# Contrast adjustment on one core: rows of 32 KB in six buffers, stores on ScalarE's queue, clip in four pieces in a written-out order

## The chip, the cores and the metric

One core of a Trainium2 chip. The metric is the device time of the program in microseconds (us); lower is better. A profile's span is a little shorter than the measured time (238.6 us against 240.2 for the kernel before).

## The reference

48 images (16 x 3) of 512 x 512 fp32 pixels, 50.33 MB in and 50.33 MB out:

```python
def reference(x, factor):            # factor = 1.5
    mean = np.mean(x, axis=(2, 3), keepdims=True)
    return np.clip(mean + factor * (x - mean), 0, 1).astype(np.float32)
```

The mean of a whole image is needed before its first pixel can be written. So a tile is read once into on-chip memory, reduced, and changed in place.

## The kernel before

A tile holds 4 images as 128 partitions x 8192 columns (4 MB); eleven such tiles, then two tiles of 2 images (2 MB). VectorE sums each row, a matmul with a block matrix gives the bias `(1 - factor) * mean` on every partition of an image, ScalarE computes `relu(factor * x + bias)`, VectorE takes the minimum with 1.

```python
TILE_IMGS = [4] * 11 + [2, 2]
X_BUFS = 5
STORE_ENGINE = "gpsimd"
# ... pools, block matrices ...
for i, N in enumerate(TILE_IMGS):
    # ... xt, src, dst ...
    nc.sync.dma_start(out=xt, in_=src)
    rsum = rpool.tile([P, 1], f32)
    nc.vector.tensor_reduce(out=rsum, in_=xt, axis=mybir.AxisListType.X, op=mybir.AluOpType.add)
    pbias = psum.tile([P, 1], f32)
    nc.tensor.matmul(pbias, blockw[N], rsum, start=True, stop=True)
    bias = bpool.tile([P, 1], f32)
    nc.scalar.copy(out=bias, in_=pbias)
    nc.scalar.activation(out=xt, in_=xt, func=mybir.ActivationFunctionType.Relu, bias=bias, scale=factor)
    nc.vector.tensor_scalar(out=xt, in0=xt, scalar1=1.0, scalar2=None, op0=mybir.AluOpType.min)
    store_eng.dma_start(out=dst, in_=xt)
```

The order on each engine is not the order of this text: the scheduler of the language chooses it.

## Time and profile before

| kernel before | |
|---|---|
| measured time | 240.24 us median of three runs (240.1 to 240.93) |
| span of the profile | 238.6 us |
| bytes moved, mean rate | 100.66 MB, 422 GB/s |
| VectorE, ScalarE busy | 66%, 37% |

From the page of the kernel before: the span cut in 40 slices (a digit is the busy share in tenths, 9 is 90% or more; GB/s is what the DMA engines moved), then the three costliest groups (line, engine, operation, output<-input, count; busy us, mean ns of one; idle time of the engine just before, and what ended it). TENSOR_REDUCE is the row sum, called reduce below; ACTIVATE is the relu; TENSOR_SCALAR is the minimum with 1, called clip; L77 is line 77 of the kernel.

```profile
DVE  0088999999599079459629909917945979742300
...
DMA  7999999999999999999999999999999999999995
GB/s 269 434 439 439 439 439 352 439 434 439 439 439 439 439 434 434 423 428 412 423 439 439 434 439 439 439 439 439 434 428 426 426 404 428 431 434 439 428 434 214
...
L77 DVE TENSOR_REDUCE rsum<-xt 128x1 f32<-128x8192 f32 (+1 forms) x13 | 104.4, 8029 | 61.7 <-DMA xt<-in_x_dram 61.7
L90 ACT ACTIVATE xt<-xt,bias 128x8192 f32<-128x8192 f32 (+1 forms) x13 | 85.8, 6598 | 0.4
L97 DVE TENSOR_SCALAR xt<-xt 128x8192 f32<-128x8192 f32 (+1 forms) x13 | 53.2, 4091 | 5.0 <-ACT xt L90 5.0
```

The DMA row is the one that is full. At 439 GB/s, the commonest value of the slices (18 of 40), 100.66 MB take 229 us, so nearly all of the 238.6 us is transfer. VectorE waits 61.7 us for loads; beyond the 13 us of the first load this costs nothing, since the DMA engines are busy meanwhile.

Why VectorE and ScalarE stay hidden can be read from the timeline of the kernel before (start us, duration us, engine, line, operation):

```profile
13.03 8.69 DVE L77 TENSOR_REDUCE rsum<-xt 128x1 f32<-128x8192 f32 x1 [13.03 <-DMA xt<-in_x_dram]
...
22.64 7.12 ACT L90 ACTIVATE xt<-xt,bias 128x8192 f32<-128x8192 f32 x1
22.73 8.69 DVE L77 TENSOR_REDUCE rsum<-xt 128x1 f32<-128x8192 f32 x1 [1.02 <-DMA xt<-in_x_dram]
31.33 4.42 DVE L97 TENSOR_SCALAR xt<-xt 128x8192 f32<-128x8192 f32 x1
...
35.66 8.68 DVE L77 TENSOR_REDUCE rsum<-xt 128x1 f32<-128x8192 f32 x1
36.06 0.67 POOL L104 DMA_DIRECT2D out_dram<-xt  x1 [34.02 <-DVE xt L97]
```

ScalarE's 7.12 us ACTIVATE of tile 0 starts at 22.64. VectorE does not wait for it: at 22.73 it reduces tile 1, and only at 31.33 clips tile 0, by which time the ACTIVATE is over. The scheduler has put reduce(t+1) ahead of clip(t). So VectorE needs 8.69 + 4.42 = 13.1 us a tile, while the 8.4 MB that a tile moves (in and out) take 19.1 us at 439 GB/s.

The end of the timeline of the kernel before:

```profile
205.31 2.46 POOL L104 DMA_DIRECT2D out_dram<-xt  x1 [9.72 <-DVE xt L97]
205.36 2.29 DVE L97 TENSOR_SCALAR xt<-xt 128x4096 f32<-128x4096 f32 x1 [0.34 <-ACT xt L90]
207.95 0.53 POOL L104 DMA_DIRECT2D out_dram<-xt  x1 [0.18 <-issue]
...
223.49 0.53 POOL L104 DMA_DIRECT2D out_dram<-xt  x1 [15.00 <-DVE xt L97]
```

The last store, of 2 MB, is issued at 223.49, when older stores are still being moved. The DMA engines never run dry. (The store's issue on GpSimd that starts at 205.31 takes 2.46 us, the others 0.53 (the first of all 0.67); a 2.29 us clip on VectorE starts just after it.)

### The profile page before, as it was taken

The page shows a single profiled execution, that of the slowest core. Times are in us where ns is not written, and L with a number is a line of the kernel's source. Part 1 is how long each engine was busy: PE and PEld are TensorE (multiplying, and loading weights), DVE is VectorE, ACT ScalarE, POOL GpSimd, SP SyncE. Part 2 cuts the span into 40 slices and gives each one's busy share as a digit, 9 for nine tenths or more (in the row PEclk, how much of TensorE's full clock was granted, in tenths as well). Part 3 has the DMA queues.
Part 4 walks back from the last instruction along what each step waited for, and adds up shares of the span by engine and source line. Part 5 has one row for each costly group of instructions (what it writes and reads, how often), then busy time and mean ns, then how long its engine had stood idle before and what let it go on. Part 6 is the DMA issues. An engine that isn't in the chain of part 4 may idle for free.

```text
span 238.6 us, 238 instructions
## 1 busy us (share of the span) xinstructions
PE 7.4 (3%) x26; PEld 6.5 (3%) x26; DVE 156.5 (66%) x26; ACT 89.1 (37%) x27; POOL 10.3 (4%) x25
## 2 busy tenths in 40 slices
PE   0000000000000000000000000000000000000000
PEld 0000000000000000000000000000000000000000
DVE  0088999999599079459629909917945979742300
ACT  2002966472906601900920650470190095406000
POOL 2000001000000000000000000000000000500000
DMA  7999999999999999999999999999999999999995
GB/s 269 434 439 439 439 439 352 439 434 439 439 439 439 439 434 434 423 428 412 423 439 439 434 439 439 439 439 439 434 428 426 426 404 428 431 434 439 428 434 214
DMA packets 3744, 100.66 MB, mean 422 GB/s; under 512 B 416, under 2 KB 416, under 8 KB 416
## 3 DMA queue, kind: packets, MB, share of 16 engines
q1 hardware_dynamic: 1872, 50.33, 49.4%
q0 software_dynamic: 1872, 50.33, 49.0%
HBM read 50.33 MB, written 50.33 MB: 422 GB/s over the span
## 4 chain that ended last, share of the span: by engine, by line
issue 38%; DMA 35%; DVE 18%; POOL 2%; POOLq 0%; SPq 0%
DMA xt<-in_x_dram 19%; DMA out_dram<-xt 16%; DVE rsum L77 11%; DVE xt L97 7%; POOL out_dram L104 2%; POOLq L137 0%; SPq L74 0%; POOLq L104 0%
## 5 line engine op out<-in xcount | busy, mean ns | idle before, releaser
L77 DVE TENSOR_REDUCE rsum<-xt 128x1 f32<-128x8192 f32 (+1 forms) x13 | 104.4, 8029 | 61.7 <-DMA xt<-in_x_dram 61.7
L90 ACT ACTIVATE xt<-xt,bias 128x8192 f32<-128x8192 f32 (+1 forms) x13 | 85.8, 6598 | 0.4
L97 DVE TENSOR_SCALAR xt<-xt 128x8192 f32<-128x8192 f32 (+1 forms) x13 | 53.2, 4091 | 5.0 <-ACT xt L90 5.0
L88 ACT COPY bias<-pbias 128x1 f32<-128x1 f32 x13 | 2.1, 160 | 130.6 <-PE pbias L85 130.6
L104 POOL DMA_DIRECT2D out_dram<-xt x13 | 9.0, 692 | 213.0 <-DVE xt L97 212.8
L85 PE MATMUL pbias<-rsum,blockw 128*128 128x1 f32 x26 | 7.4, 355 | 209.5 <-DVE rsum L77 209.5
L85 PEld LDWEIGHTS pbias<-rsum,blockw 128*128 128x128 f32 x26 | 6.5, 311 | 210.3 <-DVE rsum L77 107.1
L88 ACT ACT_TABLE_LOAD x1 | 1.3, 1283 | 0.8 <-PEq L123 0.8
L51 POOL MEMSET blockw<- 32x32 f32 (+1 forms) x6 | 0.8, 128 | 0.2
L49 POOL MEMSET blockw<- 128x128 f32 x2 | 0.3, 205 | 0.3 <-POOLq L123 0.3
L123 POOL MEMSET const-float32-0.0<- 128x1 f32 x1 | 0.1, 104 | 0.2 <-issue 0.2
L123 POOL MEMSET const-bfloat16-1.0<- 128x1 bf16 x1 | 0.1, 113 | 0.0
L123 POOL MEMSET const-uint8-127<- 128x1 uint8 x1 | 0.1, 113 | 0.0
L123 POOL MEMSET const-float32-1.0<- 128x1 f32 x1 | 0.1, 110 | 0.0
## 6 DMA issues: line engine op xcount, KB each, us to landing
xt<-in_x_dram SPq DMA_DIRECT2D x11, 4096.0 KB, 24.6
out_dram<-xt POOLq DMA_DIRECT2D x11, 4096.0 KB, 36.0
xt<-in_x_dram SPq DMA_DIRECT2D x2, 2048.0 KB, 19.5
out_dram<-xt POOLq DMA_DIRECT2D x2, 2048.0 KB, 19.1
```

The source lines that it names most:

```text
L49: nc.gpsimd.memset(wt, 0.0)
L51: nc.gpsimd.memset(wt[b * PPI : (b + 1) * PPI, b * PPI : (b + 1) * PPI], wconst)
L77: nc.vector.tensor_reduce(out=rsum, in_=xt, axis=mybir.AxisListType.X, op=mybir.AluOpType.add,)
L85: nc.tensor.matmul(pbias, blockw[N], rsum, start=True, stop=True)
L88: nc.scalar.copy(out=bias, in_=pbias)
L90: nc.scalar.activation(out=xt, in_=xt, func=mybir.ActivationFunctionType.Relu, bias=bias, scale=factor,)
L97: nc.vector.tensor_scalar(out=xt, in0=xt, scalar1=1.0, scalar2=None, op0=mybir.AluOpType.min,)
L104: store_eng.dma_start(out=dst, in_=xt)
L123: nc = _bacc.Bacc("TRN2", target_bir_lowering=False, num_devices=1)
```

## The change

The intent as far as the code shows it: one more buffer, stores issued by a second hardware queue, and a clip in pieces so that VectorE clips a piece while ScalarE is at the next. The order is written out by hand, and each engine is held to it. The core of the diff:

```diff
-TILE_IMGS = [4] * 11 + [2, 2]
-X_BUFS = 5
-STORE_ENGINE = "gpsimd"
+P = 128
+ROW = 8192
+BUFS = 6
+CHUNK = 2048
 ... (pools and block matrix cut)
+    def load(t):
+        xt = xpool.tile([P, ROW], f32, name="xt")
+        nc.sync.dma_start(out=xt, in_=dram(x_f, t))
+        tiles[t] = xt
+    def compute(t):
+        xt = tiles[t]
+        ... (rsum, matmul, bias as before)
+        for c in range(0, ROW, CHUNK):
+            part = xt[:, c : c + CHUNK]
+            nc.scalar.activation(out=part, in_=part, func=Act.Relu, bias=bias, scale=factor)
+            nc.vector.tensor_scalar(out=part, in0=part, scalar1=1.0, scalar2=None, op0=Alu.min)
+    def store(t):
+        nc.scalar.dma_start(out=dram(out_f, t), in_=tiles.pop(t))
+    with tc.manual_schedule():
+        for t in range(min(BUFS, n_tiles)):
+            load(t)
+        for t in range(n_tiles):
+            compute(t)
+            store(t)
+            if t + BUFS < n_tiles:
+                load(t + BUFS)
```

There are now 12 tiles of 4 MB, so the last store is 4 MB. In the part cut here, the pools for sum, bias and matmul result also shrink (from 12, 12 and 8 buffers to 2 each).

More of the change, by code (lines that the diff above doesn't have):

```diff
@@ L5 @@
 import concourse.tile as tile
-from concourse import bass_utils, mybir
+from concourse import mybir
 from concourse._compat import with_exitstack
-TILE_IMGS = [4] * 11 + [2, 2]
-X_BUFS = 5
-STORE_ENGINE = "gpsimd"
+P = 128
+ROW = 8192
+BUFS = 6
+CHUNK = 2048
 @with_exitstack
@@ L23 @@
     nc = tc.nc
-    P = 128
+    f32 = mybir.dt.float32
+    Alu = mybir.AluOpType
+    Act = mybir.ActivationFunctionType
     B, C, H, W = x.shape
-    n_img = B * C
-    n_pix = H * W
+    n_img, n_pix = B * C, H * W
+    ppi = n_pix // ROW
+    per_tile = P // ppi
+    n_tiles = n_img // per_tile
+    assert ppi * ROW == n_pix and per_tile * n_tiles == n_img
     factor = float(factor)
-    f32 = mybir.dt.float32
-    assert sum(TILE_IMGS) == n_img
-    NMAX = max(TILE_IMGS)
+    wconst = (1.0 - factor) / float(n_pix)
@@ L36, with dram @@
     x_f = x.rearrange("b c h w -> (b c h w)")
     out_f = out.rearrange("b c h w -> (b c h w)")
-    wconst = (1.0 - factor) / float(n_pix)
+    def dram(ap, t):
+        return bass.AP(tensor=ap.tensor, offset=t * P * ROW, ap=[[ROW, P], [1, ROW]])
     consts = ctx.enter_context(tc.tile_pool(name="consts", bufs=1))
-    blockw = {}
-    for N in sorted(set(TILE_IMGS)):
-        wt = consts.tile([P, P], f32, name=f"blockw{N}")
-        PPI = P // N
-        if N == 1:
-            nc.gpsimd.memset(wt, wconst)
-        else:
-            nc.gpsimd.memset(wt, 0.0)
-            for b in range(N):
-                nc.gpsimd.memset(wt[b * PPI : (b + 1) * PPI, b * PPI : (b + 1) * PPI], wconst)
-        blockw[N] = wt
@@ L54 @@
-    xpool = ctx.enter_context(tc.tile_pool(name="xpool", bufs=X_BUFS))
-    rpool = ctx.enter_context(tc.tile_pool(name="rpool", bufs=12))
-    bpool = ctx.enter_context(tc.tile_pool(name="bpool", bufs=12))
-    psum = ctx.enter_context(tc.tile_pool(name="psum", bufs=8, space=bass.MemoryType.PSUM))
-    if STORE_ENGINE == "sync":
-        store_eng = nc.sync
-    elif STORE_ENGINE == "act":
-        store_eng = nc.scalar
-    else:
-        store_eng = nc.gpsimd
-    pix_off = 0
-    for i, N in enumerate(TILE_IMGS):
-        FREE = n_pix * N // P
-        npix_tile = n_pix * N
-        xt = xpool.tile([P, NMAX * n_pix // P], f32, name="xt")[:, :FREE]
-        src = bass.AP(tensor=x_f.tensor, offset=pix_off, ap=[[FREE, P], [1, FREE]])
-        dst = bass.AP(tensor=out_f.tensor, offset=pix_off, ap=[[FREE, P], [1, FREE]])
-        nc.sync.dma_start(out=xt, in_=src)
-        rsum = rpool.tile([P, 1], f32)
-        nc.vector.tensor_reduce(
-            out=rsum,
-            in_=xt,
-            axis=mybir.AxisListType.X,
-            op=mybir.AluOpType.add,
-        )
-        pbias = psum.tile([P, 1], f32)
-        nc.tensor.matmul(pbias, blockw[N], rsum, start=True, stop=True)
-        bias = bpool.tile([P, 1], f32)
-        nc.scalar.copy(out=bias, in_=pbias)
-        nc.scalar.activation(
-            out=xt,
-            in_=xt,
-            func=mybir.ActivationFunctionType.Relu,
-            bias=bias,
-            scale=factor,
-        )
-        nc.vector.tensor_scalar(
-            out=xt,
-            in0=xt,
-            scalar1=1.0,
-            scalar2=None,
-            op0=mybir.AluOpType.min,
-        )
-        store_eng.dma_start(out=dst, in_=xt)
-        pix_off += npix_tile
@@ new lines @@
+    xpool = ctx.enter_context(tc.tile_pool(name="xpool", bufs=BUFS))
+    rpool = ctx.enter_context(tc.tile_pool(name="rpool", bufs=2))
+    bpool = ctx.enter_context(tc.tile_pool(name="bpool", bufs=2))
+    psum = ctx.enter_context(tc.tile_pool(name="psum", bufs=2, space=bass.MemoryType.PSUM))
+    blockw = consts.tile([P, P], f32, name="blockw")
+    nc.gpsimd.memset(blockw, 0.0)
+    for a in range(0, P, ppi):
+        nc.gpsimd.memset(blockw[a : a + ppi, a : a + ppi], wconst)
+    tiles = {}
@@ new lines, in load @@
+    def load(t):
[4 more added lines that the diff above has]
+        xt = tiles[t]
+        rsum = rpool.tile([P, 1], f32, name="rsum")
+        nc.vector.tensor_reduce(out=rsum, in_=xt, axis=mybir.AxisListType.X, op=Alu.add)
+        pbias = psum.tile([P, 1], f32, name="pbias")
+        nc.tensor.matmul(pbias, blockw, rsum, start=True, stop=True)
+        bias = bpool.tile([P, 1], f32, name="bias")
+        nc.scalar.copy(out=bias, in_=pbias)
+        for c in range(0, ROW, CHUNK):
+            part = xt[:, c : c + CHUNK]
+            nc.scalar.activation(out=part, in_=part, func=Act.Relu, bias=bias, scale=factor)
+            nc.vector.tensor_scalar(out=part, in0=part, scalar1=1.0, scalar2=None, op0=Alu.min)
```

## The prediction

> **What bounds the kernel now.** The DMA engines: the page's slice rows show DMA at 9 tenths in 38 of 40 slices and mostly 439 GB/s; 100.66 MB at 439 GB/s is 229 us of the 238.6 us span. The rest is start and tail: the last store (2 MB) is issued at 223.5, the span ends 15 us later. VectorE (66% busy) and ScalarE (37%) are hidden: the scheduler puts reduce(t+1) before clip(t); in the timeline the reduce at 22.73 runs beside ScalarE's 7.12 us ACTIVATE of the tile before, and the clip follows at 31.33. VectorE needs 8.69 + 4.42 = 13.1 us a tile; the 8.4 MB of a tile take 19.1.
>
> **What the change does.**
> 1. A sixth buffer: DMA is already full; worth about 0.
> 2. Stores on ScalarE's queue: the Trainium skill, "DMA: Bandwidth & Descriptors", section "Issuing engines are not separate DMA queues", says all issuers share the same 16 engines; this trace agrees so far as two queues together fill 98.4% of them. Under 1 us.
> 3. 12 tiles of 4 MB: the last store is 4 MB, not 2.
> 4. The written order: VectorE does reduce(t), four clips of t, then reduce(t+1). Clips wait for ScalarE, which waits for reduce(t). The overlap of reduce(t+1) with ACTIVATE(t) is gone; VectorE becomes one serial chain.
>
> **The chain per tile**, from the trace's durations:
> - reduce 8.69;
> - reduce end to ACTIVATE start, through PE and bias copy: 0.9;
> - four ACTIVATEs of 2048 columns: 7.12 us for 8192 and 3.71 for 4096 give 0.30 + 0.833 ns per column, so 2.00 each, about 7.7 in a row. The Trainium skill, "ScalarE: Activation LUTs", section "What ACT_TABLE_LOAD costs", gives 93 ns overlap of consecutive ACTIVATEs; nothing here shows it;
> - the last clip: 4.42 and 2.29 us give 0.17 + 0.52 ns per column, so 1.23.
>
> Sum: 18.5 us a tile (estimate), just under the 19.1 of DMA, so loads, six tiles ahead, should not starve it, but nothing absorbs start and end: 13.0 (first load) + 12 x 18.5 = 235 us to the last clip, then a 4 MB store with nothing to overlap: about 12 us (12.2 is the quickest landing in the trace), plus 1.3 to the end of the span as before: span 248.5. Measured time was 1.6 above the span: **250 us**. All added time is critical; the loads finish near 200 us and DMA gets idle after.
>
> **Predicted: 250 us, 8 in 10 between 246 and 256. Faster by over 2%: 0.04; within 2%: 0.08; slower: 0.88.**
>
> **What would show each step.** Reduces about 18.5 us apart, not waiting for loads after the first; VectorE idle 4 to 5 us a tile for ScalarE, some 2.9 before the first clip and 0.65 before each other. The chain of waits made of VectorE and ScalarE pieces, ending in one 4 MB store of about 12 us. Mean about 405 GB/s, full early, gaps after 200 us. Clips 48 x 1.23, ACTIVATEs 48 x 2.0.
>
> **What would make it wrong.** If dependences are kept per tile, not per piece, each ACTIVATE waits for the clip before it: 22 to 23 us a tile, about 300 us. If reduce(t+1) still gets ahead of clips of t, the kernel stays DMA bound at about 240 to 243. If the two hardware queues share bandwidth badly, a late load adds a few us. Each 0.1 us more per piece adds up to 5 us.

## The result, and the profile after

| | before | after |
|---|---|---|
| measured time, median of four runs | 240.17 us (239.85 to 240.93; the three above and one more) | 248.49 us (248.45 to 248.51) |
| ratio, 95% interval | | 1.0342 (1.032 to 1.0365) |
| span of the profile | 238.6 us | 246.7 us |
| mean rate | 422 GB/s | 408 GB/s |
| VectorE idle for loads | 61.7 us | 13.1 us (the first load alone) |
| VectorE idle for ScalarE | 5.0 us | 59.5 us |

A ratio is the mean time of one kernel's fast runs over that of the other's in the same rounds, so not quite the ratio of the medians quoted. The changed kernel is 3.4% slower. From its page:

```profile
DVE  0085695695695695695695695695695695695600
ACT  2003903903903903903803803803804804804800
...
DMA  7999999999999999999999999999999999987087
GB/s 282 436 441 452 425 351 420 441 446 446 452 425 425 425 425 425 425 430 452 446 452 430 425 425 425 426 425 425 446 442 441 446 425 430 425 345 340 0 361 319
...
L67 DVE TENSOR_REDUCE rsum<-xt 128x1 f32<-128x8192 f32 x12 | 104.1, 8679 | 13.1 <-DMA xt<-in_x_dram 13.1
L75 DVE TENSOR_SCALAR xt<-xt 128x2048 f32<-128x2048 f32 x48 | 58.9, 1227 | 59.5 <-ACT xt L74 59.5
L74 ACT ACTIVATE xt<-xt,bias 128x2048 f32<-128x2048 f32 x48 | 92.2, 1990 | 0.4
```

VectorE's idle time has changed its owner: 61.7 us waiting for loads became 13.1, and 5.0 us waiting for ScalarE became 59.5. Its busy time is about the same (156.5 us before, 162.1 after). The DMA row is full up to slice 35 and has a zero in slice 38: there the engines stood still.

One tile of the changed kernel, from its timeline:

```profile
86.94 8.68 DVE L67 TENSOR_REDUCE rsum<-xt 128x1 f32<-128x8192 f32 x1
...
96.55 7.68 ACT L74 ACTIVATE xt<-xt,bias 128x2048 f32<-128x2048 f32 x4
98.58 1.23 DVE L75 TENSOR_SCALAR xt<-xt 128x2048 f32<-128x2048 f32 x1 [2.97 <-ACT xt L74]
100.48 1.23 DVE L75 TENSOR_SCALAR xt<-xt 128x2048 f32<-128x2048 f32 x1 [0.67 <-ACT xt L74]
102.37 1.23 DVE L75 TENSOR_SCALAR xt<-xt 128x2048 f32<-128x2048 f32 x1 [0.67 <-ACT xt L74]
104.26 1.23 DVE L75 TENSOR_SCALAR xt<-xt 128x2048 f32<-128x2048 f32 x1 [0.66 <-ACT xt L74]
105.41 8.68 DVE L67 TENSOR_REDUCE rsum<-xt 128x1 f32<-128x8192 f32 x1
```

VectorE reduces until 95.62, waits 2.97 us for the bias and the first ACTIVATE, and 0.67 before each further clip. Only then comes the next reduce, 18.47 us after the one before. While VectorE reduces, ScalarE has nothing to do, and during the four ACTIVATEs (7.68 us together) VectorE waits for about half of the time. No reduce but the first waits for a load, so it is this chain, not the DMA, that sets the pace: 13.13 + 12 x 18.47 = 234.8 us to the end of the last clip, and the trace has 234.76.

What that does to the DMA engines, in three stretches at the end of the changed kernel (start:end us and length; busy us of PE, PEld, VectorE, ScalarE and GpSimd, each with its instructions; clock; DMA share; GB/s):

```profile
216.00:226.40 10.40, 0.56 (x2) 0.50 (x2) 8.88 (x2) 0.74 (x2) 0.00 (x0) 1.00 0.95 406
226.40:234.80 8.40, 0.00 (x0) 0.00 (x0) 4.91 (x4) 7.10 (x4) 0.00 (x0) 1.00 0.00 0
234.80:246.70 11.90, 0.00 (x0) 0.00 (x0) 0.00 (x0) 0.00 (x0) 0.00 (x0) 1.00 0.82 352
```

From 226.4 to 234.8 us no data start to move: all loads are done (the load queue has moved its last data by about 203 us), all stores of earlier tiles too, and the last tile is not clipped yet. Then its 4 MB go out alone; the store lands (is complete) 11.1 us after its issue. The view books a whole packet (the piece, here of 32 KB, in which data are moved) at its start. By the start and end of the packets in the trace, the DMA engines stand still from 227.07 to 235.63 us. This hole is 8.6 us long, and the kernel lost 8.3 us (248.49 less 240.17); the kernel before has no such hole.

The pages say the same in another way. Their lines for the DMA queues give packets, MB and the share of the span that the packets took, first of the kernel before, then of the changed one:

```profile
q1 hardware_dynamic: 1872, 50.33, 49.4%
q0 software_dynamic: 1872, 50.33, 49.0%
...
q1 hardware_dynamic: 1728, 50.33, 47.9%
q10 hardware_dynamic: 1728, 50.33, 47.3%
```

Before, 98.4% of 238.6 us is 234.8 us; after, 95.2% of 246.7 us is 234.9. The DMA engines worked equally long in both kernels; what was added to the span is time in which they stood still.

### The profile page after: what moved, and what is told of

It is laid out like the page before. It is cut to its first block, busy times and chain, and to the rows that moved or that the text cites. A ratio compares the mean times of both kernels' runs of the same rounds, so it can differ in the third digit from the quotient of the medians.

```text
span 246.7 us, 298 instructions
## 1 busy us (share of the span) xinstructions
PE 6.7 (3%) x24; PEld 6.0 (2%) x24; DVE 162.1 (66%) x60; ACT 95.4 (39%) x61; POOL 0.9 (0%) x9
## 4 chain that ended last, share of the span: by engine, by line
DVE 43%; ACT 34%; issue 9%; DMA 5%; PE 3%; DVEq 0%
DVE rsum L67 42%; ACT xt L74 34%; DMA xt<-in_x_dram 5%; PE pbias L69 3%; DVE xt L75 1%; ACT bias L71 1%; DVEq L75 0%
## 5 line engine op out<-in xcount | busy, mean ns | idle before, releaser
L67 DVE TENSOR_REDUCE rsum<-xt 128x1 f32<-128x8192 f32 x12 | 104.1, 8679 | 13.1 <-DMA xt<-in_x_dram 13.1
L75 DVE TENSOR_SCALAR xt<-xt 128x2048 f32<-128x2048 f32 x48 | 58.9, 1227 | 59.5 <-ACT xt L74 59.5
L74 ACT ACTIVATE xt<-xt,bias 128x2048 f32<-128x2048 f32 x48 | 92.2, 1990 | 0.4
L69 PE MATMUL pbias<-rsum,blockw 128*128 128x1 f32 x24 | 6.7, 350 | 218.9 <-DVE rsum L67 218.9
L69 PEld LDWEIGHTS pbias<-rsum,blockw 128*128 128x128 f32 x24 | 6.0, 312 | 219.5 <-issue 201.6
L55 POOL MEMSET blockw<- 32x32 f32 x4 | 0.5, 117 | 0.2
```

The lines of the kernel that those rows point to most:

```text
L55: nc.gpsimd.memset(blockw[a : a + ppi, a : a + ppi], wconst)
L69: nc.tensor.matmul(pbias, blockw, rsum, start=True, stop=True)
L74: nc.scalar.activation(out=part, in_=part, func=Act.Relu, bias=bias, scale=factor)
L75: nc.vector.tensor_scalar(out=part, in0=part, scalar1=1.0, scalar2=None, op0=Alu.min)
```

## The experiments

Theory: the written order put reduce(t+1) behind clip(t) and so made one serial chain of VectorE and ScalarE; the start and end of that chain are not covered by transfers, and that is the whole loss. Rivals: (A) the queue, the sixth buffer or the 4 MB last store cost the time; (B) the pieces do, by the fixed part of 48 ACTIVATEs and 48 clips. Each run was compared with the kernel before on the same chip; its median there was 240.04 us for the first four runs and 239.98 for the other four. Differences from the changed kernel are taken to its 248.49 us; it was not run again beside these, but the run with five buffers, which shows the same waits, took 248.49 too.

### The reduce one tile ahead, all else as changed (e1_reduce_ahead)

```diff
... (compute split into mean, contrast and clip)
+        mean(0)                      # reduce and matmul
         for t in range(n_tiles):
-            compute(t)
+            contrast(t)              # bias copy and the four ACTIVATEs
+            if t + 1 < n_tiles:
+                mean(t + 1)
+            clip(t)                  # the four clips
             store(t)
```

> The changed kernel with one thing undone: VectorE does reduce(t+1) before the four clips of tile t. My theory (the written order made one serial chain of VectorE and ScalarE, and that alone costs the time): reduces are no longer 18.47 us apart but follow the loads, DMA is full again to the end, and the time falls to 236 to 241 us, at or below the kernel before (240.2). Rival A (the two hardware queues, the sixth buffer or the 4 MB last store cost the 8 us): it stays at 245 us or above. Rival B (cutting the tile in pieces costs the time, by the fixed part of 48 ACTIVATEs and 48 clips): it stays near 248.

Measured: 239.47 us, ratio to the kernel before 0.9974 (0.9948 to 0.9999). From its page:

```profile
DVE  0088999999599189359639809917944972994400
...
DMA  7999999999999999999999999999999999999996
GB/s 265 441 441 441 441 441 353 441 441 435 430 430 424 402 435 441 441 441 441 441 441 435 424 424 419 419 435 442 437 441 441 441 430 435 424 419 419 435 441 265
...
L69 DVE TENSOR_REDUCE rsum<-xt 128x1 f32<-128x8192 f32 x12 | 104.2, 8684 | 60.2 <-DMA xt<-in_x_dram 60.2
```

One steady tile from its timeline:

```profile
136.70 7.68 ACT L81 ACTIVATE xt<-xt,bias 128x2048 f32<-128x2048 f32 x4
...
142.24 8.69 DVE L69 TENSOR_REDUCE rsum<-xt 128x1 f32<-128x8192 f32 x1 [6.14 <-DMA xt<-in_x_dram]
150.84 4.62 DVE L87 TENSOR_SCALAR xt<-xt 128x2048 f32<-128x2048 f32 x4
...
155.49 0.34 ACTq L90 DMA_DIRECT2D out_dram<-xt  x1
```

The reduce starts at 142.24, when its load has landed, without waiting for the end of the ACTIVATEs; the four clips follow without a gap in 4.62 us; VectorE waits for loads again (60.2 us in all), and the DMA row is full up to slice 39, as before the change. The order alone takes back all of the 8 us, with the queue, the six buffers, the smaller pools, the 4 MB tail and the pieces left as they are. Rivals A and B are refuted as the cause of the loss. Against the kernel before, this version gains a quarter of a per cent, if anything (the interval reaches 0.9999): both keep the DMA engines busy for over 98% of the span.

### Stores back on GpSimd's queue (e2_gpsimd_stores)

```diff
-        nc.scalar.dma_start(out=dram(out_f, t), in_=tiles.pop(t))
+        nc.gpsimd.dma_start(out=dram(out_f, t), in_=tiles.pop(t))
```

> The changed kernel with its stores back on GpSimd's queue, nothing else. My theory: the chain does not touch the queue except at the last store, so 248 to 250 us, with the reduces still 18.47 us apart. Rival A (the store queue costs the time, by ScalarE's issue or by two hardware queues sharing badly): 240 to 243 us.

Measured: 249.71 us, ratio 1.0401. As expected, the chain is unmoved (the last two reduces are 18.46 us apart). The queue is worth about 1.2 us in the changed kernel, and in ScalarE's favour: it is not what costs the time. The two traces show where: the last store is issued at 235.28 in place of 234.79, lands in 11.3 us in place of 11.1, and from the landing to the end of the span it is 1.3 us in place of 0.8.

### The clip in one piece (e3_one_piece)

```diff
-CHUNK = 2048
+CHUNK = 8192
```

> The changed kernel with the tile clipped in one piece of 8192 columns. My theory: the chain is 8.69 + 0.9 + 7.12 + 4.42 less 0.1 overlap = 21.05 us a tile in place of 18.47, so 12 x 2.6 = 31 us more: 277 to 282 us, reduces 21.05 us apart. Rival B (pieces cost the time): it gets faster than 248.5, since 36 ACTIVATEs and 36 clips with 0.3 and 0.17 us of fixed cost each are gone.

Measured: 280.06 us. The reduces are 21.04 us apart (34.15 and 55.19), as the sum of durations said. The pieces save 31.6 us in this order: without them the written order would have cost 17% instead of 3.4%. Rival B has the sign wrong.

### The kernel before, VectorE held to the written order (e5_before_written_order)

```diff
     pix_off = 0
+    order = ctx.enter_context(tc.manual_schedule(engines={mybir.EngineType.DVE}))
```

> The kernel before with VectorE alone held to the order in which the program is written (reduce, clip, reduce, clip), nothing else: still GpSimd stores, 5 buffers, whole tiles, two small tiles at the end. My theory: 13.0 + 11 x 21.05 + 2 x 11.3 (half tiles: 4.42 + 0.9 + 3.71 + 2.29) = 267 us to the last clip, then a 2 MB store of about 7 us, 1.3 to the end of the span and 1.6 to the measured time: 274 to 280 us. Rival A (queue, buffers, tail): it stays at 240.

Measured: 277.58 us, ratio 1.1563. Nothing but VectorE's order differs from the kernel before, and VectorE's wait for ScalarE goes from 5.0 to 97.8 us, its wait for loads from 61.7 to 12.9. The clip's line of its page:

```profile
L98 DVE TENSOR_SCALAR xt<-xt 128x8192 f32<-128x8192 f32 (+1 forms) x13 | 53.3, 4099 | 97.8 <-ACT xt L91 97.8
```

The order is enough to make the chain, in either kernel.

### The last store in four pieces (e6_last_store_pieces)

```diff
     def store(t):
-        nc.scalar.dma_start(out=dram(out_f, t), in_=tiles.pop(t))
+        xt = tiles.pop(t)
+        if t == n_tiles - 1:
+            for c in range(0, ROW, CHUNK):
+                nc.sync.dma_start(out=dram(out_f, t)[:, c : c + CHUNK], in_=xt[:, c : c + CHUNK])
+        else:
+            nc.scalar.dma_start(out=dram(out_f, t), in_=xt)
```

> The changed kernel with only the last tile's store cut into four stores of 1 MB, each as soon as its clip is done, on SyncE's queue (idle by then). My theory: the DMA engines stand still from 226.7 us to 234.8 in the changed kernel, waiting for the last clip, and then take 10.6 us for the 4 MB store alone. With pieces the first 3 MB go out during the last three clips, and 1 MB is left (about 2.4 + 1.1 us): some 7 us less, 240.5 to 242.5 us, the chain itself unmoved (last clip ends near 234.8). Rival (the 8 us come from lower DMA rates spread over the run, not from the end): the time falls by under 2 us.

Measured: 243.22 us, 5.3 less than the changed kernel, a little above the expected range. The hole of the changed kernel (226.4 to 234.8), cut in two stretches in this run:

```profile
226.40:229.30 2.90, 0.00 (x0) 0.00 (x0) 1.23 (x1) 2.90 (x2) 0.00 (x0) 1.00 0.00 0
229.30:234.80 5.50, 0.00 (x0) 0.00 (x0) 3.68 (x3) 4.08 (x3) 0.00 (x0) 1.00 0.92 381
```

After the first clip of the last tile (it ends at 228.97) transfers resume: by the packets at 229.84 us, 5.8 us earlier than the 235.63 of the changed kernel, and the hole is 2.9 us in place of 8.6. From there to the end of the span it is 0.5 us more than in the changed kernel, which leaves the gain of 5.3. The expectation had counted only the last 1 MB after the last clip; but the clips are 1.89 us apart and 1 MB takes some 2.5 us (10.2 for the four), so the pieces queue, and what counts is when transfers resume. The rival (under 2 us) is refuted; the gain was expected at some 7 us, too large by 1.7. These four stores also go by SyncE's queue in place of ScalarE's; no run parts that from the pieces.

### The first load and reduce in four pieces (e7_first_load_pieces)

```diff
     def load(t):
         xt = xpool.tile([P, ROW], f32, name="xt")
-        nc.sync.dma_start(out=xt, in_=dram(x_f, t))
+        if t == 0:
+            for c in range(0, ROW, CHUNK):
+                nc.sync.dma_start(out=xt[:, c : c + CHUNK], in_=dram(x_f, t)[:, c : c + CHUNK])
+        else:
+            nc.sync.dma_start(out=xt, in_=dram(x_f, t))
 ... (in compute)
-        rsum = rpool.tile([P, 1], f32, name="rsum")
-        nc.vector.tensor_reduce(out=rsum, in_=xt, axis=mybir.AxisListType.X, op=Alu.add)
         pbias = psum.tile([P, 1], f32, name="pbias")
-        nc.tensor.matmul(pbias, blockw, rsum, start=True, stop=True)
+        step = CHUNK if t == 0 else ROW
+        for c in range(0, ROW, step):
+            rsum = rpool.tile([P, 1], f32, name="rsum")
+            nc.vector.tensor_reduce(out=rsum, in_=xt[:, c : c + step], axis=mybir.AxisListType.X, op=Alu.add)
+            nc.tensor.matmul(pbias, blockw, rsum, start=c == 0, stop=c + step == ROW)
```

> The changed kernel with only the first tile's load and reduce cut into four pieces (1 MB loads, four partial sums added up by the matmul). My theory: the chain starts earlier, the first mean is ready at 13.1 + 2.3 = 15.4 us in place of 21.8, so each later step of the chain comes 6.3 us earlier: 241.5 to 243 us, reduces from the second on still 18.47 us apart, the hole in the DMA shrunk from 8 us to about 2. Rival (DMA rate, not the chain): unchanged at 248.

Measured: 244.19 us, 4.3 less than the changed kernel, where 5.5 to 7 were expected. VectorE's timeline in this run:

```profile
5.67 2.29 DVE L74 TENSOR_REDUCE rsum<-xt 128x1 f32<-128x2048 f32 x1 [5.67 <-DMA xt<-in_x_dram]
...
25.17 8.68 DVE L74 TENSOR_REDUCE rsum<-xt 128x1 f32<-128x8192 f32 x1
...
154.37 8.68 DVE L74 TENSOR_REDUCE rsum<-xt 128x1 f32<-128x8192 f32 x1
...
172.97 8.69 DVE L74 TENSOR_REDUCE rsum<-xt 128x1 f32<-128x8192 f32 x1
...
192.31 8.69 DVE L74 TENSOR_REDUCE rsum<-xt 128x1 f32<-128x8192 f32 x1 [0.78 <-DMA xt<-in_x_dram]
...
211.67 8.69 DVE L74 TENSOR_REDUCE rsum<-xt 128x1 f32<-128x8192 f32 x1 [0.80 <-DMA xt<-in_x_dram]
...
229.00 1.23 DVE L81 TENSOR_SCALAR xt<-xt 128x2048 f32<-128x2048 f32 x1 [0.66 <-ACT xt L80]
```

The second reduce starts at 25.17, 6.4 us earlier than in the changed kernel (31.61 there), as expected. But from 154.37 on the reduces are 18.6, 19.3 and 19.4 us apart, and two of them wait for a load: the pace is that of the loads by then, which end 19.3 to 19.4 us apart, near the 19.1 us of transfers a tile. The last clip ends at 230.23, 4.5 us earlier than in the changed kernel; by the packets the hole is 4.2 us in place of 8.6, and that is the gain.

The expectation failed where it left the loads where they were. In the changed kernel the last load has moved its data at 203.4 us, 12.8 before its reduce (216.21): there was a lead. In this run the first store is issued at 25.28 in place of 31.72, and the loads from the fourth tile on end 6.1 to 6.6 us later than there (the last at 209.9). The likely reason is that loads and stores share DMA engines that are full, so that earlier stores push the loads back and the lead is used up; no run tests this alone.

### Both ends in pieces (e8_both_ends)

The two edits above together.

> Both ends cut in pieces, written order kept. My theory: the two gains do not add (6.3 + 7.1 would give 235), because the DMA engines are then full to the end: 238 to 240 us, as good as the version with the reduce put ahead (239.5) and the kernel before (240.0). Should it fall to 236 or below, the limit of the DMA engines is lower than I read from the page.

Measured: 240.02 us, ratio 0.9995 (0.9969 to 1.002), at the upper edge of the expected range. From its page:

```profile
DMA  7999999999999999999999999999999999999997
GB/s 260 428 457 440 352 440 440 440 440 440 440 440 435 435 418 402 424 440 440 440 440 440 440 440 440 431 425 407 418 435 440 440 435 440 440 435 440 381 377 310
```

No slice is empty any more, and the packets leave no hole. The two gains, 5.3 and 4.3 us, would add up to 9.6; 8.5 are seen, about the length of the hole (8.6). When the hole is closed, the DMA engines are the limit again, at the time of the kernel before, with the serial order still in place. So the order costs time only through the start and the end that it leaves uncovered.

### Five buffers (e9_five_buffers)

```diff
-BUFS = 6
+BUFS = 5
```

> The changed kernel with 5 buffers in place of 6. My theory: loads are far ahead of the chain, so nothing changes: 248 to 249.5 us, no reduce but the first waits for a load. Rival (the sixth buffer does harm by letting loads take bandwidth from stores): 246 us or less; rival (the sixth buffer is what keeps the chain fed): over 252 us with reduces waiting for loads.

Measured: 248.49 us, the same as with six. From its page:

```profile
L67 DVE TENSOR_REDUCE rsum<-xt 128x1 f32<-128x8192 f32 x12 | 104.2, 8680 | 13.1 <-DMA xt<-in_x_dram 13.1
L75 DVE TENSOR_SCALAR xt<-xt 128x2048 f32<-128x2048 f32 x48 | 58.9, 1227 | 59.5 <-ACT xt L74 59.5
```

The same waits, to the tenth of a microsecond: the sixth buffer does nothing here, for good or ill.

## Why the prediction was right

The prediction was 250.0 us (246 to 256), slower at 0.88; measured were 248.49 us. Its mechanism held at each step that the experiments could touch:

- **What bounds the kernel before** is the DMA. Confirmed by the version with the reduce ahead (239.47) and the one with both ends in pieces (240.02): two different kernels, both with full DMA rows, end within 0.3% of it.
- **The written order makes a serial chain.** Confirmed in both directions: taking the order back in the changed kernel removes the loss; putting it into the kernel before adds 37.5 us.
- **The size of the chain.** Predicted 18.5 us a tile, measured 18.47; idle before the clips predicted 2.9 and 0.65, measured 2.97 and 0.67; clips predicted 1.23, measured 1.227; ACTIVATEs predicted 2.00, measured 1.990. The 93 ns by which the Trainium skill ("ScalarE: Activation LUTs", "What ACT_TABLE_LOAD costs") lets consecutive ACTIVATEs overlap is now shown: four of 1.990 us take 7.68 us in a row, so (4 x 1.990 - 7.68) / 3 = 0.093 us each.
- **The sixth buffer and the store queue are worth about nothing.** Confirmed: 0.0 and 1.2 us. The latter is a little more than the "under 1 us" of the text, since the end is uncovered.
- **The term that was mis-sized** is the end: "a 4 MB store with nothing to overlap: about 12 us ... plus 1.3". From the issue of that store to the end of the span it was 11.9 us, not 13.3. The 12.2 behind the first number was the first load's, with four more loads queued behind it; the lone store landed in 11.1 us. The 1.3 was read where GpSimd issued the stores; with ScalarE's queue it is 0.8.
- **One statement was wrong in its timing**: "the loads finish near 200 us and DMA gets idle after". The loads did finish near 203 us, but the stores, which had shared the engines with them, were behind and kept the DMA nearly full up to 227 us. There is one hole of 8.6 us, not a thin stretch from 200 us on. The predicted time did not rest on this.

That the loss is the same as the hole is shown by three runs: each time came down by about what the hole was shortened (5.7 us and 5.3; 4.3 and 4.3; 8.6, all of it, and 8.5). What stays open is the quarter of a per cent between the version with the reduce ahead and the kernel before: it has another queue, other tile sizes and other pieces, and no run parts these.

## What to carry to other kernels

When an engine works twice on each tile, with another engine's work between the two, give it the next tile's first part before this tile's second part; in the order of the loop body it waits out the other engine's time once per tile. Cutting the middle part in pieces shortens such a wait but does not remove it (21.04 to 18.47 us a tile here, against 8.68 + 4 x 1.227 = 13.6 us of VectorE's own work). And a chain that is a little faster per tile than the transfers is not free: its start and its end are added to the time unless transfers cover them, so look for slices in which the DMA row is empty, and compare their length with the loss.

## What the Trainium skill lacked or had wrong

- "Perfetto Trace Analysis", section "Optimization Strategy", says of the same gap repeating on the engine that should be saturated that it can mean too few buffers or too little memory. Here VectorE, whose chain set the pace, showed gaps of about 2.97 and three times 0.67 us in every tile; going from five to six buffers changed nothing (248.49 us both), and another order of the instructions on VectorE removed nearly all of them (59.5 to 4.6 us). The section does not name instruction order as a cause.
- "SBUF — State Buffer", section "Summary: rules for kernel authors", tells one to estimate HBM transfers at about 358 GB/s, half of what two cores share. That would give 281 us for the 100.66 MB of this kernel, which runs on one core; the trace of the kernel before shows 439 GB/s in 18 of 40 slices and 422 as a mean. The rule does not say that it is for two cores at work; the skill does not lack this altogether, since "Perfetto Trace Analysis", section "Roofline", says so and lets one core alone pull more.
- Not wrong, and one event here fits it: "SBUF — State Buffer", section "Who interferes with whom", says that VectorE in its two-port modes, which `tensor_scalar` can enter, and GpSimd block each other. In the kernel before, the one store issue on GpSimd that met a 2.29 us clip took 2.46 us in place of 0.53; with VectorE held to the written order, no issue meets a clip and all but the first (0.67) take 0.53. By the record the issue started 0.05 us before the clip, so which of the two held the other is not shown. It cost nothing there, since the DMA engines had older stores to move.
